# Splitting product 2 of two pairs into seven half-size products, and forming the sums of gate weights by an adding DMA

## The chip, the cores and the metric

The kernel runs on one core of a Trainium2 chip, in one launch. The metric is the device time of one execution in microseconds (us). A core has engines that work beside each other: TensorE (PE, matmuls; PEld is its loading of weights), VectorE (DVE, element-wise work on two operands), ScalarE (ACT, copies, casts and activation functions), GpSimd (POOL), and SyncE (SP), which here only issues DMAs. Each takes its instructions in a fixed order and waits on semaphores for the others. SBUF is the on-chip memory that they read; matmuls add up their results in PSUM, which has 8 banks of 512 floats in each of 128 partitions. SP and POOL both issue DMAs.

## The reference

Two layers. Each is a mixing part (gated linear attention beside softmax attention) and then a gated feed-forward part with a causal convolution between the up projection and the gate. The change lies in the second part, which is in outline:

```
h = rms_norm(x, ffn_norm)                 # 1040 tokens (16 learned, 1024 given), width 1024
u, g = split(h @ w_up)                    # 2816 columns each: 22 blocks of 128
u, g = causal_conv3(u), causal_conv3(g)   # depthwise, width 3
x = x + (u * silu(g)) @ w_down
```

All is float32.

## The kernel before, in words

**Numbers as pairs.** A float32 operand is split into hi (a cast by ACT) and lo (the rest, a subtraction by DVE). A product of two such operands is three matmuls, hi by hi, lo by hi and hi by lo, added up in PSUM (`mm3`, L222 to L224). The weights are the stationary operand (a tile of 128x128), the tokens the moving one (260 columns in layer 0, 258 in layer 1).

**The up projection.** `ffn_up` goes over 22 pairs j: 128 columns of u and the same 128 of g. A pair is a 2x2 problem: its weights are four blocks A11, A12 (u, lower and upper half of the inner dimension), A21, A22 (g), the tokens are halved in the same way (inner dimension by token half), and the whole is done by seven products instead of eight, in the scheme of Strassen and Winograd. Product p of pair j, written (j, p), is 4 inner tiles by 2 column groups by 3, that is 24 matmuls. Its moving operand X[p] is made once per layer. Its weight operand is

- p=1: A11, p=2: A12, p=4: A22, as they are loaded (L1045);
- p=5: S1 = A21 + A22; p=6: S2 = S1 - A11; p=7: A11 - A21; p=3: A12 - S2.

`block_operand` (L1037) loads the blocks and forms the sums, by one DVE operation of 128x512 each (L1055). For the first five pairs of a layer S1 isn't added by DVE: A21 is loaded a second time (L1048, issued by SP), and a DMA that POOL issues adds A22 to it on its way into SBUF (L1049). `up_split` (L1067) then makes hi (ACT, L1072) and lo (DVE, L1073), in two sets of three buffers that alternate, so that the operand of one product can be split when the product six places before it has ended. The blocks A11 and A12 lie in a ring of 4 buffers ("raw"), A21, A22, S1 and S2 in one of 7 ("raw2"). The p=3 combination is written over A12.

**Evacuation.** (j,1) goes into a two-bank tile "a" of PSUM and is copied by ACT to the u half of token half 0 (L1264); products 6, 7 and 4 add onto the same tile, and each partial sum is copied when it stands: this is the chain of the scheme. (j,5) and (j,3) use a tile "x", (j,2) a tile "y"; these are added by DVE to what was copied (L1263, adds of 128x520). After (j,3) come the convolution of u and of g (`conv`: one ACT operation L1252 and two DVE operations L1256 each), silu (ACT, L1283), the product (DVE, L1287), and a DMA that POOL issues, which writes the result to device memory (`actd`, L1288). PSUM is full: two tiles for "a" in turn, one for "x", one for "y" (`place`).

**Order.** PE's order is written out by hand, in the list `seq` (L1101 to L1107): from pair 5 on it is (j,2), (j,6), (j,5), (j,7), (j+1,1), (j,4), (j,3). Operands are asked for AHEAD=4 places before they are used. The orders of the other engines come from a planner, which places each instruction by estimated costs; at run time the orders are fixed.

**The end of the stage.** The down projection follows on PE without a break. Its operands (written results read back, split, and for a group of 8 blocks combined into seven moving operands) are prepared in pieces, as SBUF slots come free (`prepare`, `pump`): with every product of the last pair its X[p] is given back (`during_last`). The down projection's `down_blocks` uses `block_operand` too.

Of the kernel before, what the change touches and what calls it, by code (L numbers as in the profile page):

```python
# [25 lines left out]
NFF = 22  # L26
# [22 lines left out]
GROUPS, LAST = (("n", 0, 3), ("s", 3, 8), ("r", 11, 4), ("r", 15, 4)), (19, 3)  # L49
HALVES, HALVES_LAST, HALVES_OUT = (0, 520, 520), (8, 524, 516), (16, 528, 512)  # L50
AHEAD = 4
NSPLIT = 4
N_DMA_SUM = 5
WARM = 12


class Slots:


    def __init__(self):  # L60
        self.free = []
        self.lent = []
# [30 lines left out]
class PsumTags:  # L93
# [3 lines left out]
    def tile(self, shape, dtype, tag, name):  # L97
        pool, bufs = self.tags[tag]
        return pool.tile(shape, dtype, tag=tag, name=name, bufs=bufs)


class Work:
# [33 lines left out]
class Kern:  # L136
# [893 lines left out]
    def up_operand(self, lyr, j, p, fw, raws, odd):  # L1030
        if (j, p) in ((2, 1), (2, 2), (3, 2), (4, 2)):
            src = fw.tile([128, 4, 128], F32, tag="raw2", name="raw2")
            self.nc.sync.dma_start(src[:], self.wm[lyr, M_UP + 2 * j][:, 4 * p - 4:4 * p, :])
            return self.up_split(src, fw, odd)
        return self.block_operand(self.wm[lyr, M_UP + 2 * j], self.wm[lyr, M_UP + 2 * j + 1], 4, j, p, fw, raws, odd, j < N_DMA_SUM)

    def block_operand(self, u, g, nk, j, p, fw, raws, odd, by_dma=False):  # L1037

        nc = self.nc
        if j not in raws:  # L1040
            q = raws[j] = {}
            for name, src, k0, own in (("A11", u, 0, True), ("A21", g, 0, False), ("A22", g, nk, False), ("A12", u, nk, True)):
                q[name] = self.wp.tile([128, 4, 128], F32, tag="raw", name="raw", bufs=4) if own else \
                    fw.tile([128, 4, 128], F32, tag="raw2", name="raw2")
                nc.sync.dma_start(q[name][:, :nk, :], src[:, k0:k0 + nk, :])  # L1045
            if by_dma:
                q["S1"] = fw.tile([128, 4, 128], F32, tag="raw2", name="raw2")
                nc.sync.dma_start(q["S1"][:], g[:, 0:4, :])  # L1048
                nc.gpsimd.dma_start(q["S1"][:], g[:, 4:8, :], accum_op=ALU.add)  # L1049
        q = raws[j]  # L1050

        def combine(out, a, b, op):
            if out not in q:
                q[out] = fw.tile([128, 4, 128], F32, tag="raw2", name="raw2")
            nc.vector.tensor_tensor(out=q[out][:, :nk, :], in0=q[a][:, :nk, :], in1=q[b][:, :nk, :], op=op)  # L1055
# [8 lines left out]
        src = q[{1: "A11", 2: "A12", 3: "A12", 4: "A22", 5: "S1", 6: "S2", 7: "A21"}[p]]  # L1064
        return self.up_split(src, fw, odd, nk)

    def up_split(self, src, fw, odd, nk=4):  # L1067
# [8 lines left out]
    def ffn_up(self, lyr, mix, hT, pp, fw, halves, o0, during_last):  # L1076
        nc, s = self.nc, self.slots
        W = halves[2]
        n = W // 2
# [9 lines left out]
        X = {}  # L1089
# [154 lines left out]
        before = {1: second_half, 2: make_t2, 7: make_t3, 8: make_n4, 11: make_t1, 14: make_b22}  # L1244


        st = {}

        def conv(hb, idx):
            t = s.get(F32, "cv")  # L1250
# [7 lines left out]
            s.put(hb)  # L1258
            return t

        def evacuate(j, p):
            q = st[j]
            add = lambda out, ps: nc.vector.tensor_tensor(out=two(out), in0=used(ps), in1=two(out), op=ALU.add)  # L1263
            copy = lambda out, bank="a": nc.scalar.copy(two(out), used(q[bank]))  # L1264
            if p in (1, 2):
                bank = "a" if p == 1 else "y"
                if "u" in q:
                    add(q["u"][:, t0], q[bank])
                else:
                    q["u"] = s.get(F32, "hu")  # L1270
                    copy(q["u"][:, t0], bank)
            elif p == 6:
                copy(q["u"][:, t1])
            elif p == 7:
                q["g"] = s.get(F32, "hg")
                copy(q["g"][:, t1])
            elif p == 4:
                copy(q["g"][:, t0])
            elif p == 3:
                add(q["u"][:, t1], q["x"])  # L1280
                u, g = conv(q["u"], j), conv(q["g"], j + NFF)
                uo, go = u[:, o0:T], g[:, o0:T]
                nc.scalar.activation(go, go, AF.Silu)  # L1283
                if j == NFF - 1:
                    self.preload = self.tc.keep_in_program_order(
                        nc.scalar.preload_act_table_set("natural_log_exp_and_others"))
                nc.vector.tensor_tensor(out=uo, in0=uo, in1=go, op=ALU.mult)  # L1287
                nc.gpsimd.dma_start(self.actd[j][:, o0:T], uo)  # L1288
                s.put(u, g)
                del st[j]  # L1290
# [364 lines left out]
    def run(self):  # L1655
# [17 lines left out]
        for lyr in range(DEPTH):  # L1673
# [9 lines left out]
            with tc.tile_pool(name=f"ffn{lyr}", bufs=1, reuse_waits="tile") as fp, \  # L1683
                    tc.manual_schedule(engines={mybir.EngineType.PE}):
                ids = s.add(fp, 6, f"e{lyr}_")
                with tc.tile_pool(name=f"ups{lyr}", bufs=1, space=PSUM, reuse_waits="tile") as pp, \
                        tc.tile_pool(name=f"up{lyr}", bufs=7, reuse_waits="tile") as fw:
# [77 lines left out]
```

## Time and profile before

| what | us |
|---|---|
| median of 3 runs | 2516.06 |
| lowest and highest run | 2515.10, 2519.42 |
| the profiled execution's own time | 2518.04 |
| its span in the profile | 2516.3 |
| PE busy | 2477.9 |
| DVE busy | 1767.2 |
| ACT busy | 1272.9 |
| up projection, layer 0 (first to last matmul) | 573.5 to 1013.1 |
| up projection, layer 1 | 1817.0 to 2260.1 |

How to read the profile: times are from the start of the span. "Busy" is the time in which an engine works on at least one instruction; matmuls overlap in PE's pipeline, so a matmul's own duration (some 280 ns) is longer than the distance between two of them (some 120 ns). For DVE and ACT as well the distance of back-to-back instructions is a little under their duration. A view of windows gives each engine's busy time in a stretch, with the number of its instructions in brackets, the granted TensorE clock (1.00 is full speed) and the share of time in which the DMA engines are busy. "Idle before, releaser" says what an engine had waited for. A line number is that of the kernel before; in the kernel after the same code stands 29 to some 100 lines further down.

### The profile page before, as it was taken

The numbers are of one execution on the slowest core, as the hardware profiler recorded it, in microseconds if no ns is written. First come the engines' busy times: TensorE is split into PE (matmuls) and PEld (weight loads), VectorE is DVE, ScalarE is ACT, GpSimd is POOL, SyncE is SP. The second block draws the span as 40 slices with busy tenths as digits, with TensorE's granted clock in tenths as the row PEclk, the third lists the DMA queues.
The fourth block names the chain that finished last, engine by engine and source line by source line (L and its number), as shares of the span: only waits on it lengthen the run. The fifth ranks groups of instructions, "written<-read, shape, count | busy, mean of one in ns | idle before, by whom it ended". The sixth has DMA issues, their size and how long they took to land.

```text
span 2516.3 us, 47049 instructions
## 1 busy us (share of the span) xinstructions
PE 2477.9 (98%) x18442; PEld 2383.8 (95%) x18442; DVE 1767.2 (70%) x3523; ACT 1272.9 (51%) x2733; POOL 385.3 (15%) x567
## 2 busy tenths in 40 slices
PE   9999999999999999999999999999999999999998
PEld 8999999999999999999999899999999999997786
DVE  8656777769877777853666666777798777787535
ACT  7346666636544445631443566665464444455312
POOL 2023433210000000100211234331100000001002
PEclk9999999999999999999999999999999999999999
DMA  3232134343322224763312222143433222258722
GB/s 133 67 88 74 44 92 133 118 130 97 119 81 81 77 77 146 193 170 106 107 57 69 74 80 78 58 153 109 142 105 101 76 79 78 80 166 186 194 56 74
DMA packets 118542, 260.94 MB, mean 104 GB/s; under 512 B 14880, under 2 KB 32544, under 8 KB 118320
## 3 DMA queue, kind: packets, MB, share of 16 engines
q1 hardware_dynamic: 93984, 182.79, 23.5%
q0 software_dynamic: 22464, 72.84, 10.4%
q8 instruction: 144, 2.36, 0.4%
q10 hardware_dynamic: 1872, 2.31, 0.3%
q14 instruction: 78, 0.64, 0.1%
HBM read 177.29 MB, written 67.81 MB: 97 GB/s over the span
## 4 chain that ended last, share of the span: by engine, by line
PE 81%; DVE 10%; ACT 4%; DMA 2%; issue 2%; SPq 0%; POOL 0%; DVEq 0%; ACTq 0%; POOLq 0%
PE up L222 11%; PE up L224 11%; PE up L223 11%; PE mm L222 7%; PE mm L224 7%; PE mm L223 7%; PE down L222 5%; PE down L223 5%; PE down L224 5%; PE av L720 3%; PE tr L694 2%; DVE S L661 1%; PE S L658 1%; ACT P L673 1%; PE S L659 1%
## 5 line engine op out<-in xcount | busy, mean ns | idle before, releaser
L222 PE MATMUL up<-x,hi 128*128 128x260 f32 (+1 forms) x2464 | 696.6, 283 | 0.0
L224 PE MATMUL up<-x,hi 128*128 128x260 f32 (+1 forms) x2464 | 695.9, 282 | 0.7 <-DVE x L1097 0.7
L223 PE MATMUL up<-x,lo 128*128 128x260 f32 (+1 forms) x2464 | 696.3, 283 | 0.0
L224 PEld LDWEIGHTS up<-x,hi 128*128 128x128 f32 x2464 | 465.3, 189 | 1.1 <-DVE x L1097 1.1
L222 PEld LDWEIGHTS up<-x,hi 128*128 128x128 f32 x2464 | 464.5, 189 | 0.4 <-DVE hu L1263 0.2
L223 PEld LDWEIGHTS up<-x,lo 128*128 128x128 f32 x2464 | 464.5, 189 | 0.1
L1073 DVE TENSOR_TENSOR lo<-raw,hi 128x512 fp32r<-128x512 f32 x364 | 247.7, 685 | 173.0 <-ACT hi L1072 172.7
L222 PE MATMUL mm<-xh,hi 128*128 128x348 f32 (+4 forms) x1056 | 362.7, 343 | 0.0
L224 PE MATMUL mm<-xl,hi 128*128 128x348 f32 (+4 forms) x1056 | 339.8, 322 | 0.0
L223 PE MATMUL mm<-xh,lo 128*128 128x348 f32 (+4 forms) x1056 | 339.4, 321 | 0.0
L1072 ACT CAST hi<-raw 128x512 fp32r<-128x512 f32 x364 | 223.6, 620 | 128.1 <-PE up L224 84.5
L222 PEld LDWEIGHTS mm<-xh,hi 128*128 128x128 f32 x1056 | 199.5, 189 | 5.2 <-issue 4.6
L223 PEld LDWEIGHTS mm<-xh,lo 128*128 128x128 f32 x1056 | 199.5, 189 | 0.7 <-issue 0.7
L224 PEld LDWEIGHTS mm<-xl,hi 128*128 128x128 f32 x1056 | 198.3, 188 | 0.4 <-issue 0.3
L189 ACT CAST hi<-raw 128x512 fp32r<-128x512 f32 (+2 forms) x168 | 97.4, 581 | 176.0 <-PE down L224 97.0
L223 PE MATMUL down<-ah,lo 128*128 128x260 f32 (+1 forms) x528 | 168.6, 319 | 0.4 <-DVE lo L191 0.3
L224 PE MATMUL down<-al,hi 128*128 128x260 f32 (+1 forms) x528 | 168.5, 319 | 0.0
L222 PE MATMUL down<-ah,hi 128*128 128x260 f32 (+1 forms) x528 | 168.2, 319 | 0.0
L673 ACT ACTIVATE P<-S,m 116x460 f32<-116x460 f32 (+2 forms) x224 | 124.8, 561 | 71.2 <-DVE m L661 67.6
L337 DVE TENSOR_TENSOR PT<-tr,PT 116x464 fp32r<-116x464 f32 (+3 forms) x240 | 122.8, 514 | 46.9 <-ACT PT L336 45.3
L1055 DVE TENSOR_TENSOR raw<-raw,raw 128x512 f32<-128x512 f32 x198 | 129.4, 684 | 17.2 <-DMA raw<-in_wd_dram 16.5
L1288 POOL DMA_DIRECT2D actd<-cv x44 | 23.6, 535 | 756.9 <-DVE cv L1287 735.9
(289 smaller groups left out, 5623.8 us busy)
## 6 DMA issues: line engine op xcount, KB each, us to landing
raw<-in_wm_dram SPq DMA_DIRECT2D x330, 256.0 KB, 2.7
raw<-in_wd_dram SPq DMA_DIRECT2D x64, 256.0 KB, 3.6
actd<-cv POOLq DMA_DIRECT2D x22, 520.0 KB, 3.0
actd<-cv POOLq DMA_DIRECT2D x22, 512.0 KB, 2.9
cb<-cd SPq DMA_DIRECT2D x16, 520.0 KB, 4.1
st<-actd SPq DMA_DIRECT2D x14, 520.0 KB, 4.9
st<-actd SPq DMA_DIRECT2D x14, 512.0 KB, 4.6
kA<-kA SPq DMA_DIRECT2D x24, 260.0 KB, 3.9
```

The costliest lines, as they stand in the source:

```text
L189: nc.scalar.copy(hi[:, :n, :], raw[:, :n, :])
L222: nc.tensor.matmul(ps, wh, xh[:, c0:c0 + n], start=first, stop=False, skip_group_check=more)
L223: nc.tensor.matmul(ps, wl, xh[:, c0:c0 + n], start=False, stop=False, skip_group_check=more)
L224: nc.tensor.matmul(ps, wh, xl[:, c0:c0 + n], start=False, stop=last, skip_group_check=more)
L337: nc.vector.tensor_tensor(out=lo, in0=src, in1=hi.bitcast(F32), op=ALU.subtract)
L658: nc.tensor.matmul(S[:rows, :n], q["qA"][e][:, qs], q["kA"][e][:, c0:k1], start=True, stop=False)
L673: nc.scalar.activation(P[:rows, :n], S[:rows, :n], AF.Exp, scale=-1.0, bias=m[:rows, nch - 1:nch], accum_out=(den if nch == 1 else d3[:row ...
L694: nc.tensor.transpose(tr[:w, 3 - j, :rows], P[:rows, o:o + w], id_)
L720: nc.tensor.matmul(av[:, a:b], w.rearrange("p a b -> p (a b)"), x, start=(t == ts[0] and part == 0 and i == 0), stop=(t == last and i == 1))
L1055: nc.vector.tensor_tensor(out=q[out][:, :nk, :], in0=q[a][:, :nk, :], in1=q[b][:, :nk, :], op=op)
L1072: nc.scalar.copy(hi[:, :nk, :], src[:, :nk, :])
L1073: nc.vector.tensor_tensor(out=lo[:, :nk, :], in0=src[:, :nk, :], in1=hi[:, :nk, :].bitcast(F32), op=ALU.subtract)
```

## The change

**Product 2 of two pairs.** For j = 6, 8, ..., 20 (eight times per layer) the products (j,2) and (j+1,2), 48 matmuls, are done as one 2x2 problem of a second level. The two pairs share the moving operand X[2]; its inner dimension (4 tiles) is halved, its column groups are the two columns of the problem, and A12 of j and of j+1 are the two rows. The same scheme of seven gives products m1 to m7, in the list (j, 20+m), each of 2 inner tiles by 1 column group by 3, that is 6 matmuls, 42 in all. Two tiles of one bank each ("s0", "s1") take the place of the two-bank tile "y"; each of the seven is added into its u by a DVE operation of 128x260 (`sub_evacuate`).

- The weights of m3, m5, m6 and m7 are formed by four DVE operations of half size (128x256), and all seven are split in half size (`sub_operand`).
- The moving operands of m4 to m7 (`Y`) are made once per layer, while pairs 4 and 5 run, by `second_level`: two DVE additions of 128x1040 (hi plus lo), four combinations of 128x520 and four splits.
- The order of a two-pair becomes m1, m2, (j,6), m6, (j+1,1), m5, (j,7), (j,5), m7, (j,4), m3, (j,3), m4, (j+1,6), (j+1,5), (j+1,7), (j+2,1), (j+1,4), (j+1,3). X[2] and Y are given back after m4 of j=20, and X[1] after (21,1). In the last pair there is no (21,2) before (21,4).

**S1 of every pair by the adding DMA.** `N_DMA_SUM` is gone: all 22 pairs of a layer load A21 twice and add A22 by the DMA that POOL issues. The DVE addition remains in `block_operand` for the down projection alone.

**p=3 is written over S2** instead of over A12, in the down projection too.

```diff
-N_DMA_SUM = 5
+SUB = 20
+FIRST_SUB = 6
-        return self.block_operand(..., j, p, fw, raws, odd, j < N_DMA_SUM)
+        if p > SUB:
+            self.block_raws(*src(j), fw, raws, True)
+            self.block_raws(*src(j + 1), fw, raws, only="A12")
+            return self.sub_operand(raws[j], raws[j + 1], p - SUB, fw, odd)
+        return self.block_operand(*src(j), p, fw, raws, odd, True)
...
+    def sub_operand(self, q, r, m, fw, odd):
+        A, B = q["A12"], r["A12"]
+        lo, hi = slice(0, 2), slice(2, 4)
+        if m == 6:
+            q["s"] = fw.tile([128, 4, 128], F32, tag="raw2", name="raw2")
+            tt(q["s"][:, lo, :], B[:, lo, :], B[:, hi, :], ALU.add)
+            tt(q["s"][:, hi, :], q["s"][:, lo, :], A[:, lo, :], ALU.subtract)
+        elif m == 7:
+            tt(q["s"][:, lo, :], A[:, lo, :], B[:, lo, :], ALU.subtract)
+        elif m == 3:
+            tt(q["s"][:, hi, :], A[:, hi, :], q["s"][:, hi, :], ALU.subtract)
...
+        if by_dma and "S1" not in q:
+            q["S1"] = fw.tile([128, 4, 128], F32, tag="raw2", name="raw2")
+            nc.sync.dma_start(q["S1"][:], g[:, 0:4, :])
+            nc.gpsimd.dma_start(q["S1"][:], g[:, 4:8, :], accum_op=ALU.add)
...
-            combine("A12", "A12", "S2", ALU.subtract)
+            combine("S2", "A12", "S2", ALU.subtract)
...
-        for j in range(3, NFF - 1):
+        for j in range(3, FIRST_SUB):
             seq += ([(j, 2)] if j > 4 else []) + [(j, 6), (j, 5), (j, 7), (j + 1, 1), (j, 4), (j, 3)]
-        seq += [(NFF - 1, p) for p in (6, 5, 7, 2, 4, 3)]
+        for j in range(FIRST_SUB, NFF, 2):
+            m = lambda i: (j, SUB + i)
+            seq += [m(1), m(2), (j, 6), m(6), (j + 1, 1), m(5), (j, 7), (j, 5), m(7), (j, 4), m(3), (j, 3)]
+            seq += [m(4), (j + 1, 6), (j + 1, 5), (j + 1, 7)] + ([(j + 2, 1)] if j + 2 < NFF else [])
+            seq += [(j + 1, 4), (j + 1, 3)]
...
+        def sub_evacuate(j, m):
+            bank = sub_bank(m)
+            to, c = {1: (j, 0), 2: (j, 0), 6: (j, 1), 3: (j, 1), 5: (j + 1, 1), 7: (j + 1, 1), 4: (j + 1, 0)}[m]
+            o = st[to]["u"][:, halves[0] + c * n:halves[0] + c * n + n]
+            nc.vector.tensor_tensor(out=o, in0=st[j]["s"][bank][:, :n], in1=o, op=ALU.add)
+        sub_bank = lambda m: 0 if m in (1, 6, 7, 4) else 1
...
+                for k in range(2):
+                    self.mm3(q["s"][sub_bank(m)][:, :n], ops[i][k], xs[k], c0, n, first and k == 0, k == 1, not first)
...
+                if (j, m) == (NFF - 2, 4):
+                    for x in X.pop(2):
+                        s.put(*x)
+                    s.put(*Y.values())
+                    pp.turn()
+                    during_last(2)
```

In the orders of the engines as built, PE has 96 matmuls fewer (16 times 6). DVE loses 34 additions of S1 (17 pairs in each of two layers); SP issues 34 loads more and POOL 34 adding DMAs more.

More of the change, by code (lines that the diff above doesn't have):

```diff
@@ new lines, in sub_operand @@
+    def sub_operand(self, q, r, m, fw, odd):
+        A, B = q["A12"], r["A12"]
+        lo, hi = slice(0, 2), slice(2, 4)
+        tt = lambda out, a, b, op: self.nc.vector.tensor_tensor(out=out, in0=a, in1=b, op=op)
+        if m == 6:
[6 more added lines that the diff above has]
+            tt(q["s"][:, hi, :], A[:, hi, :], q["s"][:, hi, :], ALU.subtract)
+        src, at = {1: (A, lo), 2: (A, hi), 3: (q.get("s"), hi), 4: (B, hi), 5: (q.get("s"), lo),
+                   6: (q.get("s"), hi), 7: (q.get("s"), lo)}[m]
+        return self.up_split(src[:, at, :], fw, odd, 2)
@@ L1037, in block_operand @@
     def block_operand(self, u, g, nk, j, p, fw, raws, odd, by_dma=False):
         nc = self.nc
[L1040 to L1049, printed above, removed]
+        self.block_raws(u, g, nk, j, fw, raws, by_dma)
@@ L1259, in conv, with second_level, whole, make @@
             return t
+        Y = {}
+        def second_level():
+            at0, at1 = slice(0, n), slice(n, W)
+            t = [half_slot("t") for _ in range(2)]
+            def whole(i):
+                return lambda: nc.vector.tensor_tensor(out=t[i].t[:, :, :W], in0=X[2][0][i].t[:, :, :W].bitcast(F32),
+                                                       in1=X[2][1][i].t[:, :, :W].bitcast(F32), op=ALU.add)
+            b11, b12, b21, b22 = (x.t[:, :, at] for x in t for at in (at0, at1))
+            def make(m, out, a, b, op):
+                def f():
+                    nc.vector.tensor_tensor(out=out, in0=a, in1=b, op=op)
+                def g():
+                    Y[m] = y = s.get(F32R, f"y{m}", (128, 4, 260))
+                    self.split(y.t[:, 0:2, :n], y.t[:, 2:4, :n], out)
+                return [f, g]
+            return [whole(0), whole(1), *make(7, b12, b22, b12, ALU.subtract), *make(6, b11, b12, b11, ALU.add),
+                    *make(5, b22, b22, b11, ALU.subtract), *make(4, b21, b21, b11, ALU.subtract),
+                    lambda: s.put(*t)]
+        def sub_moving(m):
+            if m in Y:
+                return [(Y[m].t[:, k, :], Y[m].t[:, 2 + k, :]) for k in range(2)], 0
+            i, c0 = {1: (0, 0), 2: (1, 0), 3: (1, n)}[m]
+            return [(X[2][0][i].t[:, k, :], X[2][1][i].t[:, k, :]) for k in range(2)], c0
+        def sub_evacuate(j, m):
[4 more added lines that the diff above has]
+        sub_bank = lambda m: 0 if m in (1, 6, 7, 4) else 1
         def evacuate(j, p):
+            if p > SUB:
+                sub_evacuate(j, p - SUB)
+                return
             q = st[j]
```

60 lines of the change are left out of this document (54 added, 6 removed).

## The prediction

> **What bounds the kernel now.** I read the page's shares and its chain first, then windows by stage, then PE's waits in the stage that changes.
>
> ```profile
> span 2516.3 us, 47049 instructions
> PE 2477.9 (98%) x18442; PEld 2383.8 (95%) x18442; DVE 1767.2 (70%) x3523; ACT 1272.9 (51%) x2733; POOL 385.3 (15%) x567
> PE 81%; DVE 10%; ACT 4%; DMA 2%; issue 2%; SPq 0%; POOL 0%; DVEq 0%; ACTq 0%; POOLq 0%
> ```
>
> PE is busy 98% of the span and makes up 81% of the chain. The stages (columns: stretch, its length, then busy time and count of PE, PEld, DVE, ACT, POOL; clock; DMA share; GB/s):
>
> ```profile
> 600.00:645.00 45.00, 45.00 (x377) 44.91 (x376) 45.00 (x62) 29.61 (x44) 3.74 (x5) 1.00 0.38 106
> 660.00:990.00 330.00, 330.00 (x2765) 330.00 (x2764) 245.42 (x315) 160.29 (x232) 9.04 (x17) 1.00 0.26 88
> 990.00:1010.00 20.00, 20.00 (x170) 20.00 (x170) 17.18 (x20) 13.04 (x17) 0.53 (x1) 1.00 0.57 184
> 1010.00:1040.00 30.00, 29.98 (x251) 29.77 (x250) 29.89 (x32) 23.54 (x33) 4.87 (x6) 1.00 0.84 192
> 1920.00:2240.00 320.00, 320.00 (x2664) 320.00 (x2663) 234.08 (x302) 152.87 (x223) 8.50 (x16) 1.00 0.27 89
> 2240.00:2262.00 22.00, 21.98 (x175) 21.38 (x174) 19.62 (x22) 13.90 (x19) 0.53 (x1) 1.00 0.55 174
> 2262.00:2300.00 38.00, 37.67 (x163) 30.21 (x162) 35.40 (x41) 28.57 (x44) 7.41 (x9) 1.00 0.88 196
> ```
>
> In the steady up projection (660 to 990, 1920 to 2240) PE has no gap, at clock 1.00, while DVE works 74 and 73% of the time. A matmul costs 330/2765 = 0.1193 us in layer 0, 320/2664 = 0.1201 in layer 1. At the border to the down projection (1010 to 1040) DVE is full too: 29.89 of 30. PE's waits, up projection and then down projection of layer 1:
>
> ```profile
> PE up L224 <- DVE x L1097: 0.5, 1, 0.5
> ```
>
> ```profile
> PE down L222 <- DVE dg L1444: 2.7, 1, 2.7
> PE down L222 <- ACT du L1445: 1.0, 1, 1.0
> PE down L223 <- DVE lo L191: 0.3, 1, 0.3
> ```
>
> So a matmul less in the steady stage is worth its whole time, as long as DVE and the DMAs keep pace; at the border DVE is the partner to watch.
>
> **The change, part by part.**
>
> *Fewer matmuls.* 16 two-pairs save 6 each: 48 x 0.1193 + 48 x 0.1201 = 11.5 us, all on PE's path.
>
> *More borders between products.* A two-pair has 5 products more, 80 in all. Seven borders a pair leave no gap in the windows above, so the low end is 0. The high end is 0.07 each, if a weight load of 189 ns (below) wasn't overlapped by the 0.12 of a matmul: 5.6. I take 0.01 each, near the windows: **+0.8**.
>
> *DVE and ACT.* Durations by line and form:
>
> ```profile
> L224 PEld LDWEIGHTS up<-x,hi 128*128 128x128 f32 x2464 | 465.3, 189 | 1.1 <-DVE x L1097 1.1
> L1073 DVE TENSOR_TENSOR lo<-raw,hi 128x512 fp32r<-128x512 f32 x364 | 247.7, 685 | 173.0 <-ACT hi L1072 172.7
> L1055 DVE TENSOR_TENSOR raw<-raw,raw 128x512 f32<-128x512 f32 x198 | 129.4, 684 | 17.2 <-DMA raw<-in_wd_dram 16.5
> L1263 DVE TENSOR_TENSOR hu<-up,hu 128x520 f32<-128x520 f32 x44 | 30.4, 692 | 0.0
> L737 DVE TENSOR_TENSOR ff<-fo,ff 116x256 f32<-116x256 f32 x32 | 13.5, 422 | 13.2 <-ACT ff L736 12.0 <-PE S L659 0.4
> L337 DVE TENSOR_TENSOR al<-st,ah 128x1040 fp32r<-128x1040 f32 x14 | 17.2, 1238 | 16.7 <-DMA st<-actd 6.4 <-ACT ah L336 5.9 <-DMA hm<-du 2.3
> ```
>
> Back to back they follow each other some 0.08 faster (the list below: 0.60 for 684). A two-pair loses two lo, two S1 sums, two adds of 520: 6 x 0.61 = 3.7 us of DVE. It gains 7 half lo, 4 half sums and 7 half adds. The nearest row to a half operation is L737, 422 ns, so 0.34 in a row: 18 x 0.34 = 6.1. DVE goes from 0.744 x 40.1 = 29.8 to 32.3 of a two-pair's 39.4 us, 82%. It still has 7 us, so this is costed at nothing; without that cover it would be 2.5 x 16 = 40 us. ACT gains about 1 us of 39 at 49%. The building of Y is once per layer 2 x 1.15 + 8 x 0.61 = 7.2 us of DVE, in pairs 4 and 5, whose idle time is 2 x 5.1 = 10.2: nothing.
>
> *A two-pair in time.* With t=0 at m1, products start at: m2 0.7, (j,6) 1.4, m6 4.3, (j+1,1) 5.0, m5 7.9, (j,7) 8.6, (j,5) 11.5, m7 14.3, (j,4) 15.1, m3 17.9, (j,3) 18.6, m4 21.5, (j+1,5) 25.1. DVE's burst after a pair's last product, as it is now:
>
> ```profile
> 754.61 1.30 DVE L1256 SCALAR_TENSOR_TENSOR cv<-hg,vec,cv 128x1039 f32<-128x1039 f32 x1 [0.47 <-ACT cv L1252]
> 755.83 0.69 DVE L1263 TENSOR_TENSOR hu<-up,hu 128x520 f32<-128x520 f32 x1
> 756.44 1.29 DVE L1256 SCALAR_TENSOR_TENSOR cv<-hg,vec,cv 128x1038 f32<-128x1038 f32 x1
> 757.65 0.68 DVE L1073 TENSOR_TENSOR lo<-raw,hi 128x512 fp32r<-128x512 f32 x1
> 758.25 1.29 DVE L1256 SCALAR_TENSOR_TENSOR cv<-hu,vec,cv 128x1039 f32<-128x1039 f32 x1
> 759.46 0.69 DVE L1263 TENSOR_TENSOR hu<-up,hu 128x520 f32<-128x520 f32 x1
> 760.07 1.29 DVE L1256 SCALAR_TENSOR_TENSOR cv<-hu,vec,cv 128x1038 f32<-128x1038 f32 x1
> 761.28 0.68 DVE L1073 TENSOR_TENSOR lo<-raw,hi 128x512 fp32r<-128x512 f32 x1
> 761.88 1.23 DVE L1287 TENSOR_TENSOR cv<-cv 128x1040 f32<-128x1040 f32 x1
> 763.03 0.68 DVE L1073 TENSOR_TENSOR lo<-raw,hi 128x512 fp32r<-128x512 f32 x1
> ```
>
> In the changed order the burst is four convolution operations (1.21), an add (0.61), two half adds (m1, m2) and a half lo (0.34), the product (1.15), then the lo of (j,7) (0.60): 8.2 us from about t=-0.4. So m1 is added by 3.0 (m6 needs its bank at 4.3), m2 by 6.1 (m5: 7.9), and lo of (j,7) is ready at 7.9 (needed 8.6, **slack 0.7**). Formerly an operand could be split five whole products ahead, 14.3 us; here the buffers that m1 gives back leave 7.9.
>
> *S1 by DMA.* Now 10 times, issued by SP (L1048), then POOL (L1049):
>
> ```profile
> L1048 SPq DMA_DIRECT2D raw<-in_wm_dram x10: 327/328/561, 555.3 to 1878.5; - x10
> DMA to landing us min/median/max: 2.5/3.4/4.2
> ```
>
> ```profile
> 601.13 0.87 POOL L1049 DMA_DIRECT2D raw<-in_wm_dram  x1 [29.52 <-DVE x L1097]
> ```
>
> ```profile
> 639.21 0.88 POOL L1049 DMA_DIRECT2D raw<-in_wm_dram  x1 [4.29 <-DVE raw L1055]
> ```
>
> ```profile
> L1049 POOL DMA_DIRECT2D raw<-in_wm_dram x10: 867/883/917, 559.4 to 1883.3; - x10
> DMA to landing us min/median/max: 3.9/4.2/4.8
> ```
>
> Each pair from 5 on gets two DMAs of 256 KB more, so 88 GB/s become about 114 and the DMA share about 0.34: 600 to 645 (0.38) is a fair sample, and the adding DMAs issued at 601.13 and 639.21 lie in it. S1 of j+1 gets the buffer that lo of (j,7) frees: SP issues at 8.0. On POOL the result of pair j-1 is queued ahead, ready at 7.2. With 0.3 between the two, S1 stands at 15.9 (14.7 to 17.3). DVE's S2 of j+1 waits for it, and queued behind that are the add of (j,5) into hg and the next lo's. The add is done at 17.1 (15.9 to 18.5); (j,3) overwrites that bank at 18.6. **Slack 1.5, at worst 0.1.** Stalls: 0 at the low end, 24 at the high (rival one); I take 0, since even the slowest landings of the trace just fit.
>
> The Trainium skill speaks against this part: "SBUF — State Buffer", section "SBUF: two separate sides", says that a DMA issued from GpSimd can't get its descriptors written while VectorE holds the shared port pair, and gives 620 ns becoming 3100. By its 2.5 us S1 would stand at 18.4, the add at 19.6, 1.0 late in each two-pair, and the sum would be 2523; the trace doesn't agree, since at 601.1 POOL issued such a DMA in 0.87 us under a VectorE that was busy 45.00 of 45, and none of the ten took over 4.8 to land.
>
> *p=3 over S2* moves no operation; A12's buffer comes free earlier, S2's later.
>
> *The border.* X[1] and X[2] are given back earlier: after (21,1) come 9 whole and 4 half products, 28.7 us, instead of 8 whole, 22.9; after m4 of j=20 come 5 whole, 14.3, where (21,2) had 2, 5.7. So down operands can be prepared sooner; but the last two-pair holds 2.5 us more DVE work, where DVE has only 2.8 + 0.1 us idle in 50 (rows 990 to 1040). PE comes to the down projection earlier and finds lo's late: 0 to 2.5 us a layer; on the other side, today's waits there (4.0 in layer 1) could go. Range -7 to +5 for both; nearest is DVE's full row, softened by the earlier hand-back: **+2.0**.
>
> Sum: -11.5 + 0.8 + 2.0 = -8.7. The profiled execution took 2518.0 (span 2516.3 and 1.7 around it), so 2509.3; the median of 2516.1 is 2.0 below it, which gives **2507.4**.
>
> **The rivals.**
>
> *One, slower: the adding DMA is late.* Slowest landings (S1 at 17.3) and one convolution operation of 1.3 us to be waited out: 18.6, the add at 19.8, 1.2 late, 16 times: 19 us, 2526. It decides from 0.54 us of stall in a two-pair on (8.7/16). For it: the median leaves 1.5 us and SP's queue must issue at once. Against it: the ten landings.
>
> *Two, same: DVE's burst is late.* Lo of (j,7) has 0.7 us; a burst 1.0 us longer (one operation of 0.6 placed in front, one ACT result 0.4 late) costs 0.3 x 16 = 5: 2512. Against it: its terms are rows.
>
> *Three, no gain: the border gives it back.* If DVE, full from 1010 to 1040, sets when the down operands stand, each layer's 5.75 us return as waits there: 2516.1 + 0.8 = 2517.
>
> *Four, more: the border is relieved* by the earlier hand-back and PE waits no more than now: 2516.1 - 10.7 = 2505; with part of today's 4 us gone, 2503.
>
> **How the numbers follow.** What a measurement here can tell from no change is about 0.2%, 5 us. Forecast 0.50 (2503 to 2511), rival four 0.12 (2502 to 2505), one 0.20 (2512 to 2531, mostly over 2521), two 0.07, three 0.11. Faster: 0.62. Same, two and three: 0.18. Slower, one: 0.20. The range 2502 to 2521 leaves out most of rival one and a little below. The forecast's own range is 2503 to 2511.
>
> **What the profile after would show.** Right: PE x18346; pairs 6 to 21 at 39.4 us per two, without PE gaps; DVE about 82% there; L1101's landings at 4 to 5 us. Wrong by rival one: in each two-pair PE waits before (j,3) on DVE's add into hg, and DVE's S2 waits on the adding DMA. By two: PE's L223 waits on lo at (j,7). By three: the up projection is 5.7 us shorter per layer but PE's waits on lo and dg in the first 50 us of the down projection grow by as much.

## The result: slower by 0.8%

The changed kernel takes 2537.5 us (median of 6 runs, 2535.9 to 2543.8), the kernel before 2518.1 (6 runs, 2515.1 to 2519.4). The ratio is 1.0081, with a 95% interval of 1.0071 to 1.0092. The forecast was 2507.4 with a range of 2502 to 2521: wrong in sign and outside the range. The profiled execution has a span of 2534.1 us, 17.8 more than before. The page of the changed kernel:

```profile
span 2534.1 us, 47524 instructions
PE 2474.9 (98%) x18346; PEld 2374.0 (94%) x18346; DVE 1820.7 (72%) x3733; ACT 1298.5 (51%) x2821; POOL 416.8 (16%) x601
PE 67%; DVE 14%; issue 7%; DMA 6%; ACT 5%; POOL 1%; SPq 0%; POOLq 0%; DVEq 0%; ACTq 0%
```

The 96 matmuls are gone (18442 to 18346), PE's busy time is 3 us less, and yet PE's share of the chain fell from 81 to 67%: DVE, the DMAs and "issue" (time for which the profile shows no wait) have entered it. Where the time went, from the starts of the matmuls in the traces (the up projection counted from its first product, some 5 us ahead of the times in the table of before):

| us | before | after |
|---|---|---|
| up projection, layer 0 | 444.7 | 449.7 |
| up projection, layer 1 | 448.1 | 448.2 |
| down projection to its last block, layer 0 | 210.4 | 216.7 |
| down projection to its last block, layer 1 | 206.2 | 211.8 |

So the up projection gave nothing where 11.5 us were due (+5.0 and +0.1 instead of -5.7 each), and the down projection lost 12.0. The windows (columns as in the prediction):

```profile
700.00:980.00 280.00, 276.19 (x2287) 273.92 (x2286) 220.83 (x347) 140.68 (x228) 20.18 (x28) 1.00 0.38 108
1930.00:2230.00 300.00, 299.29 (x2480) 298.41 (x2479) 237.53 (x372) 152.56 (x247) 20.69 (x29) 1.00 0.36 105
998.00:1018.00 20.00, 18.46 (x148) 17.66 (x147) 19.75 (x26) 12.73 (x18) 0.55 (x1) 1.00 0.78 249
1018.00:1045.00 27.00, 25.18 (x208) 24.76 (x207) 27.00 (x27) 21.55 (x31) 4.62 (x6) 1.00 0.66 141
```

In layer 0 PE is idle 3.8 of 280 us where before it had no gap, while DVE is busy only 79% of the time. An engine with 21% to spare makes PE wait. DVE's own waits in 700 to 980 (us in total, times, longest) and its order in one two-pair (j=8, whose m1 starts at 737.1) say why:

```profile
DVE raw L1112 <- DMA raw<-in_wm_dram: 34.5, 8, 5.0
```

```profile
749.71 0.43 DVE L1130 TENSOR_TENSOR lo<-raw,hi 128x256 fp32r<-128x256 f32 x1 [1.08 <-ACT hi L1129]
754.35 0.69 DVE L1112 TENSOR_TENSOR raw<-raw,raw 128x512 f32<-128x512 f32 x1 [4.22 <-DMA raw<-in_wm_dram]
754.96 0.69 DVE L1364 TENSOR_TENSOR hg<-up,hg 128x520 f32<-128x520 f32 x1
...
760.10 1.29 DVE L1317 SCALAR_TENSOR_TENSOR cv<-hg,vec,cv 128x1039 f32<-128x1039 f32 x1
761.31 0.68 DVE L1130 TENSOR_TENSOR lo<-raw,hi 128x512 fp32r<-128x512 f32 x1
761.91 0.69 DVE L1364 TENSOR_TENSOR hu<-up,hu 128x520 f32<-128x520 f32 x1
```

L1112 is S2 of pair 9. It waits 4.2 us for the sum S1 by DMA. Behind it come the add into hg (754.96) and then 7 us of work with one pause of 0.15, until the add into hu at 761.91, which PE needs before (9,5) can overwrite its bank. PE's waits in 660 to 1018:

```profile
PE up L251 <- DVE hu L1364: 2.8, 8, 0.6
PE up L251 <- DVE hg L1364: 1.8, 4, 0.5
PE up L251 <- ACT hg L1365: 0.7, 1, 0.7
```

The sum itself was asked for when forecast (its base was issued at t=8.0 in nearly every two-pair), but it stood at t=16.7 to 18.0 instead of 15.9. Base (L1100) and adding DMA (L1101) in the changed kernel:

```profile
L1100 SPq DMA_DIRECT2D raw<-in_wm_dram x44: 327/328/1359, 555.9 to 2241.3; - x44
DMA to landing us min/median/max: 2.4/3.7/5.5
```

```profile
L1101 POOL DMA_DIRECT2D raw<-in_wm_dram x44: 864/884/914, 560.1 to 2247.3; - x44
DMA to landing us min/median/max: 3.7/4.3/5.9
```

```profile
749.39 0.89 POOL L1101 DMA_DIRECT2D raw<-in_wm_dram  x1 [4.08 <-ACT hg L1365]
752.80 0.88 POOL L1101 DMA_DIRECT2D raw<-in_wm_dram  x1 [2.51 <-DMA raw<-in_wm_dram]
```

```profile
745.13 0.33 SPq L1100 DMA_DIRECT2D raw<-in_wm_dram  x1
746.36 2.02 SPq L1097 DMA_DIRECT2D raw<-in_wm_dram  x3
748.66 0.33 SPq L1100 DMA_DIRECT2D raw<-in_wm_dram  x1
```

For j=8 the base was issued at 745.13 and landed 3.7 later, POOL issued 0.6 after that, and the sum landed another 4.9 later, with four more loads issued within 3.9 us. Over the two-pairs the whole took 8.9 to 10.0 us for the pair j+1, median 9.3, where 7.9 had been taken from the ten cases of before.

The gaps between matmuls of the up projection (what a distance of over 0.15 us has beyond 0.12) add up to 23.1 us over both layers, against 7.0 before: some 11.5 inside the two-pairs, some 2.4 more than before at the start of the stage, most of it at (1,6), and 1.9 before (21,4), which has no (21,2) in front of it any more and waits for ACT's copy of (21,7).

In the down projection PE waits at three places in layer 0. Before there were two, shorter ones (first the lines of before, then of the changed kernel):

```profile
PE down L222 <- DVE dg L1444: 1.9, 1, 1.9
PE down L222 <- ACT du L1445: 1.0, 1, 1.0
```

```profile
PE down L251 <- DVE dg L1572: 3.1, 1, 3.1
PE down L252 <- DVE lo L220: 1.7, 1, 1.7
PE down L251 <- ACT du L1573: 1.7, 1, 1.7
```

That is 6.5 us of waits instead of 2.9. Another 1.7 of the 6.3 that this stage lost are matmuls at about twice their usual distance, at a lower granted clock (2.0 us instead of 0.3; the last section shows such a stretch).

### The profile page after: what moved, and what is told of

Read it like the earlier page. It is cut to its first block, busy times and chain, and to the rows that moved or that the text cites. A ratio compares the mean times of both kernels' runs of the same rounds, so it can differ in the third digit from the quotient of the medians.

```text
span 2534.1 us, 47524 instructions
## 1 busy us (share of the span) xinstructions
PE 2474.9 (98%) x18346; PEld 2374.0 (94%) x18346; DVE 1820.7 (72%) x3733; ACT 1298.5 (51%) x2821; POOL 416.8 (16%) x601
## 4 chain that ended last, share of the span: by engine, by line
PE 67%; DVE 14%; issue 7%; DMA 6%; ACT 5%; POOL 1%; SPq 0%; POOLq 0%; DVEq 0%; ACTq 0%
PE mm L251 7%; PE mm L253 7%; PE mm L252 7%; PE up L251 6%; PE up L252 6%; PE up L253 6%; DMA raw<-in_wm_dram 4%; PE down L251 4%; PE down L252 4%; PE down L253 4%; PE av L749 3%; PE tr L723 2%; DVE cv L1317 2%; DVE lo L1130 2%; DVE S L690 1%
## 5 line engine op out<-in xcount | busy, mean ns | idle before, releaser
L251 PE MATMUL up<-x,hi 128*128 128x260 f32 (+1 forms) x2208 | 627.0, 284 | 8.7 <-DVE hu L1364 4.3
L252 PE MATMUL up<-x,lo 128*128 128x260 f32 (+1 forms) x2208 | 624.0, 283 | 1.6 <-DVE lo L1130 1.6
L253 PE MATMUL up<-x,hi 128*128 128x260 f32 (+1 forms) x2208 | 623.4, 282 | 0.1
L251 PEld LDWEIGHTS up<-x,hi 128*128 128x128 f32 x2208 | 416.3, 189 | 13.7 <-issue 6.7
L252 PEld LDWEIGHTS up<-x,lo 128*128 128x128 f32 x2208 | 416.4, 189 | 2.0 <-DVE lo L1130 1.9
L253 PEld LDWEIGHTS up<-x,hi 128*128 128x128 f32 x2208 | 416.9, 189 | 0.4 <-DVE x L1154 0.3
L1130 DVE TENSOR_TENSOR lo<-raw,hi 128x512 fp32r<-128x512 f32 (+1 forms) x444 | 268.1, 617 | 95.3 <-ACT hi L1129 94.6
L1129 ACT CAST hi<-raw 128x512 fp32r<-128x512 f32 (+1 forms) x444 | 244.5, 565 | 176.3 <-DVE raw L1112 84.3
L1112 DVE TENSOR_TENSOR raw<-raw,raw 128x512 f32<-128x512 f32 x164 | 109.5, 685 | 74.1 <-DMA raw<-in_wm_dram 68.7
L749 PE MATMUL av<-PT,V 116*128 116x256 f32 (+4 forms) x768 | 130.7, 280 | 1.5 <-DVE PT L366 0.8
```

The costliest lines, as they stand in the source:

```text
L251: nc.tensor.matmul(ps, wh, xh[:, c0:c0 + n], start=first, stop=False, skip_group_check=more)
L252: nc.tensor.matmul(ps, wl, xh[:, c0:c0 + n], start=False, stop=False, skip_group_check=more)
L253: nc.tensor.matmul(ps, wh, xl[:, c0:c0 + n], start=False, stop=last, skip_group_check=more)
L749: nc.tensor.matmul(av[:, a:b], w.rearrange("p a b -> p (a b)"), x, start=(t == ts[0] and part == 0 and i == 0), stop=(t == last and i == 1))
L1129: nc.scalar.copy(hi[:, :nk, :], src[:, :nk, :])
L1130: nc.vector.tensor_tensor(out=lo[:, :nk, :], in0=src[:, :nk, :], in1=hi[:, :nk, :].bitcast(F32), op=ALU.subtract)
```

## The experiments

**S1 of pairs 6 to 21 by DVE.** The two-pairs stay.

```diff
-            self.block_raws(*src(j), fw, raws, True)
+            self.block_raws(*src(j), fw, raws, j < FIRST_SUB)
-        return self.block_operand(*src(j), p, fw, raws, odd, True)
+        return self.block_operand(*src(j), p, fw, raws, odd, j < FIRST_SUB)
```

> S1 of pairs 6 to 21 is added by DVE again, all else is as in the changed kernel. Theory A (the sum by the adding DMA lands some 9.3 us after its base was issued, 1.4 later than was allowed, and DVE, which waits for it with everything behind it, makes PE wait in each two-pair): the some 11 us of PE's waits inside the two-pairs go, the losses at the start of the up projection and in the down projection stay: about 2526 where before is 2518. Rival B (DVE has too much to do in a two-pair, late landings or not): DVE gets two operations more in each two-pair, 1.2 us, and the waits stay or grow: 2537 or more.

Measured: 2519.5, ratio to before 1.0020 (1.0011 to 1.0030); before was 2514.5 in this comparison. Windows:

```profile
700.00:980.00 280.00, 280.00 (x2343) 280.00 (x2342) 238.56 (x370) 146.60 (x234) 7.44 (x14) 1.00 0.27 88
1930.00:2230.00 300.00, 300.00 (x2496) 300.00 (x2495) 249.84 (x388) 154.92 (x250) 7.98 (x15) 1.00 0.26 85
```

DVE has more to do (85% instead of 79%) and PE has no gap at all in these stretches. Theory A holds, rival B falls: it was not the amount of DVE's work. The up projection takes 441.2 and 444.2 us, 3.5 and 3.9 less than before the change; the down projection stays long (217.7 and 207.7). Against 2526 expected it came out lower relative to before: 5.0 above it instead of 8, mostly from layer 1's down projection.

**S1 without the addition.**

```diff
-            nc.gpsimd.dma_start(q["S1"][:], g[:, 4:8, :], accum_op=ALU.add)
+            if j < FIRST_SUB:
+                nc.gpsimd.dma_start(q["S1"][:], g[:, 4:8, :], accum_op=ALU.add)
```

> S1 of pairs 6 to 21 is only the plain load of A21; the adding DMA is left out (this leaves out part of the computation), DVE's work is that of the changed kernel. Theory A: S1 stands 5 us earlier, PE's waits inside the two-pairs go: about 2526. Rival B: DVE has the same work in the same time, so the waits stay: 2537. If it comes out faster than the run with S1 by DVE, DVE's 1.2 us per two-pair count too.

Measured: 2519.3, ratio 1.0016 (1.0006 to 1.0026). In 700 to 980 PE is busy 280.00 of 280 with DVE's work unchanged, and the up projection takes 441.2 and 444.5. With the same operations in DVE's queue the waits go when the adding DMA does. Whether its landing or its load on the DMA queues is the harm, this run doesn't tell; the run with the base of S1 loaded first does. It is no faster than the run before, so DVE's 1.2 us per two-pair didn't count there.

**The adding DMA for all pairs, in the kernel before.**

```diff
-N_DMA_SUM = 5
+N_DMA_SUM = NFF
```

> The kernel before with S1 of all pairs by the adding DMA and nothing else changed: whole products, p=3 over A12. If the adding DMA does harm by itself (landings, queues), PE waits appear in each pair and the time is over 2525. Theory A says that it does harm only where the buffer for it comes free as late as in the two-pair: here S1 is asked for a whole pair ahead, no waits in the up projection, 2516 to 2520; the border, where DVE is full, may gain 1 to 2 us.

Measured: 2520.3, ratio 1.0021 (1.0012 to 1.0031), just past the upper end of what A gave, and 5.8 us slower than before (2514.5 in this comparison), where A allowed about 2. In steady pairs there is no gap (280.00 of 280), as A has it: the base is issued 0.5 us after (j,6) starts and the sum stands at 8.3 to 9.4. But at pair 4, just before the first pair that got its S1 from DVE before, PE waits 1.6 and 0.9 us, and the down projection of layer 0 takes 1.9 more. So this part of the change brings nothing even where its landing is hidden.

**p=3 over A12 again.**

```diff
-            combine("S2", "A12", "S2", ALU.subtract)
-        src = q[{1: "A11", 2: "A12", 3: "S2", 4: "A22", 5: "S1", 6: "S2", 7: "A21"}[p]]
+            combine("A12", "A12", "S2", ALU.subtract)
+        src = q[{1: "A11", 2: "A12", 3: "A12", 4: "A22", 5: "S1", 6: "S2", 7: "A21"}[p]]
```

> The changed kernel with p=3 written over A12 as before (up and down projection). Theory C (S2 held longer is what makes the down projection 12 us longer): at least half of it returns, 2530 or less. Rival D (the down projection is late because DVE, full at the border, makes its operands late): the down projection stays some 12 us longer than before, 2535 to 2539. The waits inside the two-pairs stay in both.

Measured: 2571.5, ratio 1.0227 (1.0212 to 1.0242). Neither side expected this. The down projection stays long (216.3 and 212.9), so theory C falls; but the up projection grows to 464.6 and 466.8. DVE's and PE's waits (DVE in 700 to 980, PE in the whole span):

```profile
DVE raw L1112 <- DMA raw<-in_wm_dram: 55.5, 19, 7.0
```

```profile
PE up L251 <- DVE hg L1364: 18.8, 8, 4.0
PE up L251 <- DVE hu L1364: 13.2, 13, 2.5
```

So writing p=3 over S2, which the prediction had costed at nothing, spares the two-pairs some 35 us. What fits: with A12 held until p=3, in a ring of four buffers of which a two-pair reads two A12 at once, the next blocks come later still. In the trace the base of S1 of pair j+2 is issued at t=14.2 to 15.4 instead of 11.3 to 11.6, and S1 of pair j+1 stands at up to 20.9 instead of 18.0. The ring of A12 was not varied by itself.

**X[2] and Y given back late** (in the kernel with S1 by DVE).

```diff
                 if (j, m) == (NFF - 2, 4):
-                    for x in X.pop(2):
-                        s.put(*x)
-                    s.put(*Y.values())
                     pp.turn()
-                    during_last(2)
                 continue
+            if (j, p) == (NFF - 1, 4):
+                for x in X.pop(2):
+                    s.put(*x)
+                s.put(*Y.values())
+                during_last(2)
```

> The kernel with S1 of pairs 6 to 21 by DVE (2519.5, where before was 2514.5), and X[2] and Y are given back only before (21,4), where X[2] was given back before the change. Theory E (the early hand-back lets the pump take more slots, so that ACT's first copies in the blocks of the down projection get a slot whose last DMA is still on its way): ACT's wait on that DMA goes, 3 to 5 us less in the down projection, about 2515. Rival D (DVE, full at the border, is late because the last two-pair gave it more work): the operands come later still, PE waits longer on lo, 2519 to 2524.

Measured: 2523.9, ratio 1.0032 (1.0021 to 1.0044), in rival D's range. The down projection takes 218.5 and 210.0, and the wait for ACT's copies grew (8.3 us in 4 times, from 5.2 in 3) instead of going; before (21,4) in layer 0 PE waits 3.3 us instead of 0.8. Theory E falls. Most of the growth is in ACT's copies and not in lo (2.1, from 2.2), so D is not shown by this run either.

**Pairs 20 and 21 with whole products** (in the kernel with S1 by DVE). `END_SUB` = 20 ends the two-pairs; the old order follows, and the exchange of the PSUM tiles comes after m4 of j=18.

```diff
+END_SUB = 20
-        for j in range(FIRST_SUB, NFF, 2):
+        for j in range(FIRST_SUB, END_SUB, 2):
...
+        for j in range(END_SUB, NFF - 1):
+            seq += [(j, 2), (j, 6), (j, 5), (j, 7), (j + 1, 1), (j, 4), (j, 3)]
+        seq += [(NFF - 1, p) for p in (6, 5, 7, 2, 4, 3)]
...
-                if (j, m) == (NFF - 2, 4):
-                    for x in X.pop(2):
-                        s.put(*x)
+                if (j, m) == (END_SUB - 2, 4):
                     s.put(*Y.values())
                     pp.turn()
-                    during_last(2)
```

> As the run with S1 by DVE, but pairs 20 and 21 are done with whole products as before: 7 two-pairs per layer, 12 matmuls more. Theories D and E both say that the end of the up projection and the down projection are then as before the change: 8.8 us of the down projection and 1.7 at (21,4) return, 1.4 are lost: about 2510. If the down projection's loss has nothing to do with the last two-pair: 2519 to 2521.

Measured: 2514.2, ratio 0.9997 (0.9987 to 1.0006); before was 2515.5 in this comparison, so the gain against before is 1.3 us where 4.5 were expected. The down projection of layer 0 is back at 210.6 (from 217.7), and the wait before (21,4) is gone; layer 1 hardly moves (207.7 to 207.4), and there the expectation failed. So in layer 0 it was the last two-pair that made the down projection late. D explains a part of it. The lines below, DVE in the changed kernel, fit D: the lo of the third weight tile stands behind four convolution operations, an add and two splits of down operands without a break, and PE waits 1.9 us for it at 1029.6.

```profile
1021.27 1.23 DVE L366 TENSOR_TENSOR x<-st,x 128x1040 fp32r<-128x1040 f32 x1
...
1027.81 1.28 DVE L1317 SCALAR_TENSOR_TENSOR cv<-hu,vec,cv 128x1038 f32<-128x1038 f32 x1
1029.02 0.54 DVE L220 TENSOR_TENSOR lo<-raw,hi 128x384 fp32r<-128x384 f32 x1
```

The second wait there, 1.9 us at 1063.2, isn't DVE's: ACT's first copy in the blocks waits for a DMA that reads the tile "do", whose slot it seems to take over. In layer 0 a wait of 1.9 to 3.3 us at this place, 43 to 46 us into the stage, stands in every kernel with the last two-pair and in none without it.

```profile
1062.57 0.59 ACT L1573 COPY du<-down 128x520 f32<-128x520 f32 x1 [5.62 <-DMA hm<-do]
```

**The same, with p=3 of pairs 0 to 5 over A12.**

```diff
-            combine("S2", "A12", "S2", ALU.subtract)
-        src = q[{1: "A11", 2: "A12", 3: "S2", 4: "A22", 5: "S1", 6: "S2", 7: "A21"}[p]]
+            combine("A12" if early else "S2", "A12", "S2", ALU.subtract)
+        src = q[{1: "A11", 2: "A12", 3: "A12" if early else "S2", 4: "A22", 5: "S1", 6: "S2", 7: "A21"}[p]]
...
-        return self.block_operand(*src(j), p, fw, raws, odd, j < FIRST_SUB)
+        return self.block_operand(*src(j), p, fw, raws, odd, j < FIRST_SUB, j < FIRST_SUB)
```

> As the run with pairs 20 and 21 whole, and p=3 of pairs 0 to 5 is written over A12 as before. Theory F (PE's wait of 1.2 us at (1,5) in each layer comes from the order that DVE gets with p=3 over S2): these 2.3 us go, 2.3 faster than the run with pairs 20 and 21 whole. If that wait has another cause: the same time.

Measured: 2515.2, ratio 0.9998 (0.9988 to 1.0007): no gain. The wait on lo is gone (it is that of (1,6); the expectation names the wrong product), so theory F holds for its cause, but 2.1 us of waits on DVE's add into hu came in its place, at (4,5), and a stretch at half the clock behind the longer one: the up projection of layer 0 takes 443.5 instead of 441.1.

**The base of S1 loaded first** (in the changed kernel, S1 by the adding DMA).

```diff
-        for name, src, k0, own in (("A11", u, 0, True), ("A21", g, 0, False), ("A22", g, nk, False), ("A12", u, nk, True)):
-            if name in q or only not in (None, name):
+        for name, src, k0, own in (("A11", u, 0, True), ("S1", g, 0, False), ("A21", g, 0, False), ("A22", g, nk, False), ("A12", u, nk, True)):
+            if name in q or only not in (None, name) or name == "S1" and not by_dma:
                 continue
...
             nc.sync.dma_start(q[name][:, :nk, :], src[:, k0:k0 + nk, :])
-        if by_dma and "S1" not in q:
-            q["S1"] = fw.tile([128, 4, 128], F32, tag="raw2", name="raw2")
-            nc.sync.dma_start(q["S1"][:], g[:, 0:4, :])
-            nc.gpsimd.dma_start(q["S1"][:], g[:, 4:8, :], accum_op=ALU.add)
+            if name == "S1":
+                nc.gpsimd.dma_start(q["S1"][:], g[:, 4:8, :], accum_op=ALU.add)
```

> The changed kernel (S1 of all pairs by the adding DMA), with the base of S1 loaded ahead of A21 and A22 of its pair, so that it gets the buffer that comes free first. Theory A: the sum stands some 3 to 4 us earlier in each two-pair, DVE's waits of 4 to 5 us shrink to about 1 and PE's waits inside the two-pairs go: about 2527. If the waits come from the load on the DMA queues or DVE rather than from when the buffer comes free: 2535 or more.

Measured: 2516.3, ratio 1.0005 (0.9996 to 1.0015): with the same instructions, the loss against before is gone. Windows, and DVE's waits at L1110 (the combinations of blocks) in 700 to 980:

```profile
700.00:980.00 280.00, 280.00 (x2343) 280.00 (x2342) 229.88 (x357) 146.65 (x234) 20.48 (x29) 1.00 0.40 116
1930.00:2230.00 300.00, 300.00 (x2497) 300.00 (x2496) 242.03 (x378) 155.37 (x250) 21.25 (x30) 1.00 0.38 114
```

```profile
DVE raw L1110 <- issue: 8.3, 6, 1.8
DVE raw L1110 <- DMA raw<-in_wm_dram: 7.1, 4, 3.6
...
DVE raw L1110 <- DVE raw L1110: 2.3, 3, 0.9
```

The profile puts 7.1 us down to DMAs, but every one of DVE's 14 pauses before L1110 there ends within 0.15 us after a landing: 34.5 us of waits became 18.4, none over 1.8 but one, and in these stretches PE doesn't wait at all. The adding DMAs follow in the order of the pairs; counted so, S1 of pair j+1 now stands 1 to 8 us before its two-pair begins instead of 17 to 18 us into it, some 20 us sooner and not the 3 to 4 that were expected. The DMAs are the same, the DMA share is 0.40 instead of 0.38, and the adds land after 3.6 to 6.6 us, median 4.2. So it was not the load on the queues, but when the buffer came free that S1 takes in the ring. In the changed kernel SP had stood waiting for that buffer, until a lo of DVE released it (SP's waits in 700 to 980):

```profile
SPq L1100 <- DVE lo L1130: 122.4, 13, 19.7
```

The gain went past what was expected (2527): the down projection gained as well (214.2 and 207.8, from 216.7 and 211.8). In layer 0 1.7 of the 2.5 us are a stretch at half the clock that this execution didn't have. That DVE comes to the border with less of a backlog is not shown: the run without the addition has no late sums either, and its down projection of layer 0 takes 218.3.

**Both: S1's base first, pairs 20 and 21 whole.** The edits are those of the last run and of the run with `END_SUB`.

> The base of S1 loaded ahead of A21 and A22 (2516.3), and pairs 20 and 21 with whole products (which took the run with S1 by DVE from 2519.5 to 2514.2). If the two losses, the late S1 in the two-pairs and DVE's load at the border, are separate and no other is large, the gains add: 2516.3 less about 5, 2511, faster than before by 0.15 to 0.2%. If the loads that the adding DMA needs are late again at the border, 2514 or more.

Measured: 2517.0, ratio 1.0006 (0.9997 to 1.0015). The gains don't add (2511 was expected). At the passage from the two-pairs to the whole ones one S1 is late again. DVE's and POOL's timelines of this run:

```profile
953.46 1.29 DVE L1111 TENSOR_TENSOR raw<-raw,raw 128x512 f32<-128x512 f32 x2 [4.57 <-issue]
```

```profile
947.83 0.87 POOL L1100 DMA_DIRECT2D raw<-in_wm_dram  x1 [8.28 <-DVE hu L1358]
```

The profile names no releaser for DVE's 4.57 us, but the adding DMA issued at 947.83 landed at 953.38. PE then waits 1.7 and 0.7 us at 958 and 962, and 0.9 and 0.7 at the same place of layer 1.

**The changed kernel with pairs 20 and 21 whole, nothing else.**

> The changed kernel with pairs 20 and 21 with whole products and nothing else. Theory A with D: the waits of the other seven two-pairs stay (10 of 11 us), the end of the up projection and the down projection are as before (some 12 of 13 us return, 1.4 are lost): about 2526. If the down projection was late because DVE came to it with a backlog from late sums, and not for the last two-pair itself, it stays late: 2535.

Measured: 2526.7, ratio 1.0041 (1.0028 to 1.0055). The up projection keeps its waits (451.7 and 447.0), the down projection of layer 0 is as before (209.7), that of layer 1 partly (209.8). The two losses are separate in layer 0.

**S1's base first, pairs 20 and 21 whole, S1 of pairs 18 to 21 by DVE.**

```diff
-            self.block_raws(*src(j), fw, raws, True)
+            self.block_raws(*src(j), fw, raws, j < 18)
-        return self.block_operand(*src(j), p, fw, raws, odd, True)
+        return self.block_operand(*src(j), p, fw, raws, odd, j < 18)
```

> As the run with S1's base first and pairs 20 and 21 whole (2517.0), but S1 of pairs 18 to 21 is added by DVE. There DVE waited 4.6 us for a sum by DMA at 953.46, at the passage from the two-pairs to the whole ones, and in layer 1 ACT 3.3 us for a block read back beside those loads. If these are what kept the gains from adding: 2511. If the passage itself (the exchange of the PSUM tiles, DVE's order) costs it: 2515 to 2517.

Measured: 2513.7, where before was 2516.7; ratio 0.9989 (0.9980 to 0.9997). It beats both kernels, by 0.1% and 0.9%, though less than expected. The up projection takes 441.1 and 443.7, the down projection 210.8 and 207.4. In the run before this one the up projection took 443.6 and 446.1: the late S1 at the passage was what kept the gains from adding.

**The same edit with all eight two-pairs.**

> As the run with S1's base first and all eight two-pairs (2516.3), but S1 of pairs 18 to 21 is added by DVE. Rival D (DVE, full at the border, sets when the down projection's operands stand): DVE gets four additions more, 2.4 us, in the last two two-pairs, and the down projection is 1 to 3 us later per layer: 2518 to 2521. If the loads of the adding DMA near the border are the harm: 2513 to 2515.

Measured: 2520.8, ratio 1.0012 (1.0003 to 1.0021), in D's range, though the interval overlaps that of the run without the four additions (0.9996 to 1.0015). The down projection is 218.2 and 211.1, against 214.2 and 207.8. Of the 4.0 us in layer 0, though, 2.7 are stretches at half the clock, and only some 1.5 are longer waits. The two runs with S1 by DVE and with the addition left out speak against reading this as D alone: the first has the same additions and 207.7 in layer 1, the second has none of them and 218.3 in layer 0. So that DVE's load at the border sets the start of the down projection fits this run, but is not shown.

## Why the prediction was wrong, point by point

- **Fewer matmuls, -11.5 us: right.** Wherever DVE wasn't late, PE ran without a gap at 0.1195 us a matmul (280/2343), and with all eight two-pairs the up projection became 2.6 to 3.9 us shorter in a layer; most of what is missing to 5.7 are the waits at (1,6) and (21,4), some 2.
- **More borders between products, +0.8: right.** There is no gap, but five two-pairs without a wait took 197.40 us in layer 0 and 198.50 in layer 1 (S1 by DVE), where ten whole pairs had taken 200.67 and 202.00: 0.3 and 0.1 less saved than 30 matmuls at their old distance, some 0.7 over both layers.
- **DVE at 82% of a two-pair, hidden: right as a sum.** 229.88/280 = 82%, and 85% with S1 by DVE, without a wait of PE. Y and the lo of (j,7), slack 0.7, caused no wait either; rival two didn't come.
- **S1 by DMA, "stalls: 0": the step that failed.** Measured: some 11.5 us of PE's waits inside the two-pairs. The chain was right to 0.1 us up to the issue of the base (t=8.0). Its landing was mis-sized: 7.9 us from the medians of before, 9.3 in the two-pairs (base 3.7 instead of 3.4, POOL's issue 0.6 instead of 0.3, the add 4.8 instead of 4.2). A part of this stood in the trace of before: POOL issues 0.6 us after the landing there too, and the ten whole chains take 7.2 to 9.2 us, median 8.4. The rest: the ten samples had come from a stage with the same mean DMA share, but in a two-pair these DMAs go out with others close by; that this is why they are slower was not tried by itself. And the price of a late sum was taken at the wrong end: only the add into hg, next in DVE's queue, was held against PE's need of it (slack 1.5; PE waited there 0.1 to 0.7 us in 7 of 16 two-pairs). What mattered as much was the 4 to 5 us that DVE stood still: the work queued up behind it, and the add into hu, 7 us later, missed (j+1,5) by 0.3 to 1.1 us in 13 of 16. Rival one had the late sum and a price of the right order (19 us were forecast for the slowest landings, some 11.5 came), but looked for the waits before (j,3), where the smaller part of them is, and was given 0.20.
- **The other objection to S1 by DMA, 2523.** 44 adding DMAs landed in 3.7 to 5.9 us, median 4.3, against 3.9 to 4.8 for ten before. So the rule of the Trainium skill ("SBUF — State Buffer", "SBUF: two separate sides": a GpSimd DMA starved of descriptors by VectorE) did not act. The sum it gave was on the right side for another reason.
- **p=3 over S2, "moves no operation": wrong by omission.** Undone, it costs some 35 us. It seems that a buffer's lifetime in a short ring is a cost or a gain of its own.
- **The border, +2.0 for both layers: mis-sized; measured +12.0.** Its upper end was 5. In layer 0 the last two-pair is the cause: without it the 6 us go. Only a part of them is the one named (DVE full, and the last two-pair gives it more): from the changed kernel to the same with pairs 20 and 21 whole, waits on DVE's lo and dg fall from 4.8 to 2.5 us, the wait of 1.7 on ACT's copy goes, and stretches at half the clock fall from 2.0 to 0.2. The copy was left out of the prediction, and so was the clock. The earlier hand-back was no harm: given back late, the stage got longer.
- **Not costed at all:** the wait before (21,4), 0.85 a layer, which the order in the diff shows; and the one at (1,6), some 1.2 a layer, that comes from another order which DVE gets.

Open: what sets the down projection of layer 1. It moved between 205.2 and 212.9 us over the kernels, and not with the last two-pair (207.7 with it and 207.4 without it, where S1 is by DVE). Part of this is the clock, below.

## What to carry to other kernels

Where an engine works in a fixed order, a wait costs all that is queued behind it: price it by the idle time that it puts into that engine and look for the tightest need in the next ten operations, not for that of the next one. When a load's start hangs on a ring of buffers, the order in which the tiles are asked for decides how early it can start; here, asking for one tile two places sooner was worth 19 us. Read the length of such a chain from whole cases and not from the medians of its steps, and from a place where the same loads go out beside it.

## What the runs showed of the hardware

After a wait of PE the granted clock sometimes falls to about half for some 3.5 us (matmuls 0.216 us apart instead of 0.120, until 1067.0 in the lines below), and whether it does isn't told by the length of the wait. In the changed kernel, stretches with two waits and what followed them (clock is the third number from the end):

```profile
1059.00:1063.00 4.00, 2.48 (x21) 2.26 (x19) 0.53 (x1) 0.43 (x1) 0.00 (x0) 1.00 1.05 267
1063.00:1067.00 4.00, 3.79 (x19) 3.79 (x19) 0.86 (x2) 1.79 (x4) 0.00 (x0) 0.57 0.89 269
...
1136.00:1140.00 4.00, 1.00 (x9) 0.80 (x7) 4.00 (x5) 1.52 (x3) 0.00 (x0) 1.00 0.94 381
1140.00:1144.00 4.00, 3.86 (x32) 3.87 (x33) 2.50 (x4) 0.00 (x0) 0.85 (x1) 1.00 0.98 299
```

A wait of 1.9 us that ended at 1063.2 was followed by a stretch of 4 us with a clock of 0.57, one of 3.3 us that ended at 1140.1 by none. A dip costs about 1.7 us (19 matmuls where 33 fit), and over the kernels a down projection lost 0 to 3.4 us to matmuls at about twice their usual distance, in no order that follows the edits: a wait of 2 us can cost 4. The Trainium skill ("TensorE: Matmul & The Clock Gate", "Part 1: The HAM clock gate") tells of a window of some 3.4 us that runs on its own and halves the clock after an idle window. The length of the dip agrees; the gap of 1.9 us before the fall is shorter than a whole idle window.
